# Two alternating groups in the chunk recurrence of a hybrid decoder layer, with copies shared by two engines

## The chip, the cores and the metric

The kernel runs on one core of a Trainium2 chip. The metric is the device time of one execution in microseconds (us). The kernel before was timed in three runs; a fourth execution was profiled.

## The reference, cut to what matters

One decoder layer on a sequence of T = 2048 tokens of width D = 1024, all in float32. Three branches (A, B, C) work on one projection of the normalised input:

```python
h = rms_norm(x, norm_g[l])
p = h @ w_in[l]
y_a = rwkv7_mix(p_r, p_k, p_v, p_w, p_a, ...) * silu(z_a)          # branch A: 8 heads x 64
y_b = sliding_window_sink_attn(p_q, p_sk, p_sv, ...) * silu(z_b)   # branch B: window 128
y_c = memory_cross_attn(p_xq, mem, ...) * silu(z_c)                # branch C: 256 memory tokens
merged = gates[0] * (y_a @ w_proj_a) + gates[1] * (y_b @ w_proj_b) + gates[2] * (y_c @ w_proj_c)
x = x + merged @ w_out
```

Branch A is a recurrence over tokens with a 64x64 state S for each head:

```python
sa = jnp.einsum('bhvk,bhk->bhv', S, a_t)
S = S * w_t[:, :, None, :] + sa[..., None] * b_t[:, :, None, :] + v_t[..., None] * k_t[:, :, None, :]
y = jnp.einsum('bhvk,bhk->bhv', S, r_t)
```

## The kernel before

**Tiling.** The sequence is cut into four blocks of 512 tokens (block 0 to block 3). Most of TensorE's time goes into projections: each 128-row block of weights is split into a high and a low part in a fast format, and three large products of 512 columns (L462 to L464, in `gemm3`) give the projection. Weights come in tiles `whl` of 512 KB, of which a ring holds nine; one tile serves twelve large products. In block 0 the raw weights (256 KB a tile) are loaded, split by ScalarE (L444, a cast) and VectorE (L445), and the split tile is written back to memory (`k`); blocks 1 to 3 load the split tiles.

**The recurrence.** Branch A is computed in chunks of 64 tokens, eight chunks in a block, for eight heads in four pairs. `rwkv_prep` makes four factors for each pair and stores them in memory (`f`); `rwkv_chain` walks through the chunks with all four pairs at once. For each chunk it loads the factors (L852, into `whl` tiles, two chunks' worth being in flight) and runs:

- L866: the W products from the state Z into a PSUM tile `rw` (8 products), L867: the part of the output that depends on Z (8 products, into `yps`);
- L869: VectorE copies W out of PSUM;
- L874: the U products from W (8 products); in odd chunks L845 adds the previous chunk's U part to the output (8 products);
- L877: VectorE copies U into Z in two halves of 64 partitions;
- L879: the S products, the new state (8 products); in odd chunks L845 again, for this chunk;
- L885: VectorE adds the decayed old state SP (made by GpSimd, L872) into a new Z, in two halves; ScalarE copies the output out of PSUM after odd chunks (L889).

Each small float32 product appears in the trace as two records. L866, L867 and L879 use TensorE in the shape 128*64, L874 and L845 in the shape 64*64, and the large products in 128*128. L861 and L862 (GpSimd) fill the halves of Z that come from the values.

**What sets the order.** The program is written as streams (recurrence `r`, attention `a`, merges `b` and `c`, gates `g`), and the letters of `TURNS` say which stream takes the next step, in block 0 and in the blocks after it. Then `order` lays the whole program out again: `lay_out` keeps one clock for each engine and always places the instruction that can start first (on a tie of candidates, the one with the lowest rank, which after the first of `PASSES` = 3 rounds is the latest time at which it is due). Each engine then executes its instructions strictly in the resulting order. `burst` chains the products of a stage behind each other, without a bond to the next stage, so that large products may stand in between. A **visit** below is an unbroken row of the recurrence's products between two other instructions of TensorE.

The order also shows the other small products of TensorE (transposes, attention, the factors' own products): they too make visits, outside the change.

## Time and profile before

| | |
|---|---|
| median of three runs | 2276.46 us (2273.06 to 2279.18) |
| profiled execution, its time | 2280.36 us |
| its span | 2278.6 us |
| recurrence, block 0 | 444 to 510 us |
| recurrence, blocks 1, 2, 3 | 1009 to 1072, 1561 to 1624, 2112 to 2176 us |

The profile has, among others, a list of the engines' busy time, the chain of waits that ended last, groups of instructions by line with their mean length, a table of who waited for whom, a timeline, and windows (stretches of the span with each engine's busy time, the clock granted to TensorE, the share of the DMA engines and what they moved). A record of a matmul is longer than the distance to the next one, since matmuls are pipelined: what a product costs TensorE is read from one start to the next. PEld are TensorE's weight loads.

### The profile page before, as it was taken

What the parts mean: (1) busy time and instruction counts of PE and PEld (TensorE: products, weight loads), DVE (VectorE), ACT (ScalarE), POOL (GpSimd) and SP (SyncE); (2) the same over time, 40 slices, a digit from 0 to 9 for tenths busy, and PEclk for the clock granted to TensorE, in tenths of its full rate; (3) what the DMA queues carried; (4) which work ended last, traced back from release to release, by engine and by line L of the source; (5) the groups of instructions that cost most, each with busy time, mean ns of one, the idle gap of its engine ahead of it and who ended that gap; (6) DMA issues with size and microseconds to landing.
All of it is one profiled execution on the core that took longest, in us unless ns stands there. A gap on an engine that the chain in (4) does not pass through costs nothing.

```text
span 2278.6 us, 38340 instructions
## 1 busy us (share of the span) xinstructions
PE 2236.3 (98%) x14088; PEld 1824.9 (80%) x14088; DVE 1468.4 (64%) x4444; ACT 835.2 (37%) x1803; POOL 212.3 (9%) x297
## 2 busy tenths in 40 slices
PE   7999999999999999999999999999999999999999
PEld 5888888877788888887888788887788878888787
DVE  6789888648468857743627876772454787765252
ACT  5555546326234343311413443421332334251030
POOL 1001000021000100101100000101200000000110
PEclk9999999999999999999999999999999999999999
DMA  7787777877866555567674554556676465546665
GB/s 244 255 273 244 253 248 264 272 249 269 304 237 191 172 171 184 168 202 251 231 245 158 185 188 168 181 170 213 238 241 222 154 193 177 168 154 210 217 216 184
DMA packets 218075, 487.81 MB, mean 214 GB/s; under 512 B 19616, under 2 KB 81440, under 8 KB 217888
## 3 DMA queue, kind: packets, MB, share of 16 engines
q1 hardware_dynamic: 205216, 462.28, 60.3%
q10 hardware_dynamic: 12672, 23.07, 3.0%
q8 instruction: 112, 1.84, 0.3%
q14 instruction: 75, 0.61, 0.1%
HBM read 357.88 MB, written 127.40 MB: 213 GB/s over the span
## 4 chain that ended last, share of the span: by engine, by line
PE 87%; DMA 5%; DVE 5%; ACT 2%; issue 1%; SPq 0%; POOL 0%; ACTq 0%; DVEq 0%
PE mm L462 21%; PE mm L463 21%; PE mm L464 21%; PE rw L758 2%; DMA whl<-in_w_in 2%; PE oo L1085 1%; PE mm L1131 1%; PE mm L1130 1%; PE mm L1132 1%; PE oo L980 1%; DMA whl<-k 1%; DMA rt<-in_x 1%; PE rw L879 1%; PE rw L866 1%; DVE whl L445 1%; PE rw L874 1%
## 5 line engine op out<-in xcount | busy, mean ns | idle before, releaser
L462 PE MATMUL mm<-hH,whl 128*128 128x512 f32 x1888 | 749.1, 397 | 7.5 <-ACT whl L444 5.6
L463 PE MATMUL mm<-hL,whl 128*128 128x512 f32 x1888 | 748.9, 397 | 0.0
L464 PE MATMUL mm<-hH,whl 128*128 128x512 f32 x1888 | 744.8, 395 | 0.0
L462 PEld LDWEIGHTS mm<-hH,whl 128*128 128x128 f32 x1888 | 355.2, 188 | 80.9 <-ACT whl L444 6.3
L463 PEld LDWEIGHTS mm<-hL,whl 128*128 128x128 f32 x1888 | 355.3, 188 | 73.4 <-issue 1.2
L464 PEld LDWEIGHTS mm<-hH,whl 128*128 128x128 f32 x1888 | 355.4, 188 | 71.3 <-DVE whl L445 1.9
L1096 ACT ACTIVATE g<-mm 128x512 f32<-128x512 f32 x96 | 57.4, 598 | 298.3 <-PE mm L464 294.7
L444 ACT ACTIVATE whl<-whl 128x512 fp32r<-128x512 f32 x174 | 109.0, 629 | 149.7 <-DMA whl<-in_w_in 95.0
L445 DVE TENSOR_TENSOR whl<-whl 128x512 fp32r<-128x512 f32 x174 | 119.3, 688 | 68.2 <-ACT whl L444 63.6
L777 DVE TENSOR_TENSOR ibc<-ibc,Yi 128x248 f32<-128x248 f32 (+30 forms) x496 | 143.7, 290 | 11.1
L776 DVE STREAM_SHUFFLE ibc<-Nc 128x248 f32<-128x248 f32 (+30 forms) x496 | 150.8, 312 | 0.1
L462 PE MATMUL mm<-yh,whl 128*128 128x512 f32 x384 | 150.0, 394 | 0.8 <-ACT yh L927 0.5
L464 PE MATMUL mm<-yh,whl 128*128 128x512 f32 x384 | 150.0, 391 | 0.8 <-DVE whl L445 0.8
L463 PE MATMUL mm<-yl,whl 128*128 128x512 f32 x384 | 149.9, 391 | 0.3 <-DVE yl L928 0.2
L778 DVE TENSOR_TENSOR Yi<-Yi,ibc 128x248 f32<-128x248 f32 (+30 forms) x496 | 140.4, 283 | 1.3
L427 POOL TENSOR_SCALAR st<-st 128x4 f32<-128x4 f32 (+1 forms) x32 | 9.7, 303 | 997.1 <-DVE st L513 955.3
L1111 DVE SCALAR_TENSOR_TENSOR g<-g,mm 128x512 f32<-128x512 f32 x64 | 43.7, 685 | 84.2 <-PE mm L464 80.9
L1065 ACT ACTIVATE g<-g,mxs,st 128x256 f32<-128x256 f32 (+1 forms) x128 | 74.4, 583 | 53.3 <-DVE mxs L1058 34.7
L462 PEld LDWEIGHTS mm<-yh,whl 128*128 128x128 f32 x384 | 72.0, 188 | 17.5 <-ACT yh L927 1.3
L463 PEld LDWEIGHTS mm<-yl,whl 128*128 128x128 f32 x384 | 72.1, 188 | 16.0 <-DVE yl L928 1.5
L464 PEld LDWEIGHTS mm<-yh,whl 128*128 128x128 f32 x384 | 72.1, 188 | 15.6 <-DVE whl L445 1.0
L1144 DVE SCALAR_TENSOR_TENSOR g<-mm,g 128x512 f32<-128x512 f32 x16 | 11.0, 690 | 83.4 <-PE mm L1132 78.0
(1734 smaller groups left out, 3492.1 us busy)
## 6 DMA issues: line engine op xcount, KB each, us to landing
whl<-k SPq DMA_DIRECT2D x474, 512.0 KB, 3.4
k<-whl SPq DMA_DIRECT2D x158, 512.0 KB, 3.2
whl<-f SPq DMA_DIRECT2D x128, 256.0 KB, 4.4
whl<-in_w_in SPq DMA_DIRECT2D x118, 256.0 KB, 3.5
f<-FT SPq DMA_DIRECT2D x48, 512.0 KB, 4.8
f<-FT SPq DMA_DIRECT2D x32, 256.0 KB, 4.1
g<-in_x ACTq DMA_DIRECT2D x32, 256.0 KB, 5.5
out<-g ACTq DMA_DIRECT2D x32, 256.0 KB, 4.2
```

The source lines that it names most:

```text
L444: S.activation(w[:, 0], raw, AF.Copy)
L445: V.tensor_tensor(w[:, 1], raw, w[:, 0].bitcast(F32), op=ALU.subtract)
L462: PE.matmul(out, lh, rh, start=i == 0, stop=False)
L463: PE.matmul(out, lh, rl, start=False, stop=False)
L464: PE.matmul(out, ll, rh, start=False, stop=i == n - 1)
L758: PE.matmul(g[:, c], BK[h, c0 + c], Q[h, c0 + c], start=True, stop=True)
L776: V.stream_shuffle(bc[:, :, :n], Nc[:, :, s + 1:], [s] * 32)
L777: V.tensor_tensor(bc[:, :, :n], bc[:, :, :n], Y[:, :, s:s + 1].to_broadcast([128, NC_, n]), op=ALU.mult)
L778: V.tensor_tensor(Y[:, :, s + 1:], Y[:, :, s + 1:], bc[:, :, :n], op=ALU.add)
L1065: S.activation(prs[b][:, i, m0:], prs[b][:, i, m0:], AF.Exp, scale=r2[:, b, i:i + 1], bias=mx[:, b, i:i + 1], accum_out=mx[:, b, 2 + i:3 + i])
L1096: S.activation(t, gp, AF.Tanh, scale=0.5)
L1111: V.scalar_tensor_tensor(g, g, 1.0, pp, op0=ALU.add, op1=ALU.mult)
```

## The change

In `rwkv_chain`, the four pairs are cut into two groups of two (A: pairs 0 and 1, B: pairs 2 and 3). Each stage is written as group A's four products, then group B's, each group with a PSUM half tile of its own and copies of its own. W is copied by ScalarE instead of VectorE (one copy of 128x128 for each group). U is copied by VectorE for the even heads and by ScalarE for the odd heads (64x128 each). The additions of the new state stay on VectorE, now four of 64x128 for each chunk instead of two of 64x256. The next chunk's Z, and GpSimd's copies into it, are made before the S products, and Z has three buffers instead of two. The tile `w4` in `rwkv_prep` has one buffer instead of two.

All of the recurrence's products of a block form one line in a fixed order (`run`, `lines`). In `lay_out`, once a product of the line is placed, its follower (`then`) is preferred: if it can start within `HOLD` = 300 ns of TensorE's clock, it is placed next and TensorE waits for it; if what it depends on isn't placed yet but another engine can place something by then, TensorE places nothing until that is done; otherwise the bond is dropped and large products come in. The planner takes 80 ns instead of 200 as the delay after a product of the line (`late`). The letters of `TURNS` are new.

Line numbers shift: L462 to L464 become L474 to L476, L444 and L445 become L456 and L457, L866 and L867 become L894 and L895, L874 becomes L903, L845 becomes L857, L879 becomes L911, L885 becomes L912, L889 becomes L922, L1096 becomes L1130. The W copy is L896, the U copies are L904 on both engines.

On TensorE, in block 1, an odd chunk of the recurrence before (names: `rw` W, U or S in PSUM, `yps` the output, `mm` a projection):

```order
L866 MATMUL rw<-Z,whl 64x64 x8
L867 MATMUL yps<-Z,whl 64x64 x8
L462 MATMUL mm<-hH,whl 128x512
L874 MATMUL rw<-W,whl 64x64 x8
L845 MATMUL yps<-Z,whl 64x64 x8
L463 MATMUL mm<-hL,whl 128x512
L464 MATMUL mm<-hH,whl 128x512
L462 MATMUL mm<-hH,whl 128x512
L879 MATMUL rw<-Z,whl 64x64 x8
L845 MATMUL yps<-Z,whl 64x64 x8
L463 MATMUL mm<-hL,whl 128x512
```

and an odd chunk of the change, from the first product of the visit:

```order
L894 MATMUL rw<-Z,whl 64x64 x4
L895 MATMUL yps<-Z,whl 64x64 x4
L894 MATMUL rw<-Z,whl 64x64 x4
L895 MATMUL yps<-Z,whl 64x64 x4
L903 MATMUL rw<-W,whl 64x64 x8
L857 MATMUL yps<-Z,whl 64x64 x8
L911 MATMUL rw<-Z,whl 64x64 x8
L857 MATMUL yps<-Z,whl 64x64 x8
L894 MATMUL rw<-Z,whl 64x64 x4
L475 MATMUL mm<-hL,whl 128x512
L476 MATMUL mm<-hH,whl 128x512
```

Before, the chunk is three visits with large products between them; now it is one visit of 52 products that ends with group A's first stage of the next chunk.

On ScalarE, in block 0, a stretch of the recurrence before (casts of weights, gates, output copies):

```order
L444 ACTIVATE whl<-whl 128x512
L889 ACTIVATE rt<-yps 128x128 x4
L444 ACTIVATE whl<-whl 128x512 x2
L1096 ACTIVATE g_5361<-mm 128x512
L444 ACTIVATE whl<-whl 128x512
L889 ACTIVATE rt<-yps 128x128 x4
L1096 ACTIVATE g_5471<-mm 128x512
L444 ACTIVATE whl<-whl 128x512 x2
```

and the beginning of the recurrence in the change:

```order
L896 ACTIVATE W<-rw 128x128
L456 ACTIVATE whl<-whl 128x512
L1130 ACTIVATE g_5140<-mm 128x512
L456 ACTIVATE whl<-whl 128x512
L896 ACTIVATE W<-rw 128x128
L904 ACTIVATE Z<-rw 64x2x64
L456 ACTIVATE whl<-whl 128x512
L904 ACTIVATE Z<-rw 64x2x64
L1130 ACTIVATE g_5188<-mm 128x512
L456 ACTIVATE whl<-whl 128x512
```

The casts of weights (now L456) stand between the new copies of W and U. In the whole recurrence of block 0 there are 16 of them between the first W copy and the last output copies.

The diff, with its two long tables of letters as they are:

```diff
--- before.py
+++ after.py
@@ -20,10 +20,11 @@
 TB = 512
 NG = 12
 NRT = 6
+HOLD = 300
 PASSES = 3
 TURNS = (
-    "rrararaaaraaabaaaaaraaabrrraaaaabacbrbgaaaararrabrbaaabraabgaaararraararcccccccrggrrgrgrrgrrrrgrrc",
-    "aarrbraraaaaraaaaaaaraaaraararbgbaaabracararabaaarrbbabraaaabararaarrgracgcccccrgrgrcrgrrgrrrrrrgc",
+    "rraaaraaaaaaabaraarraaabrarraaaabraabbgaaarcarrbrraaaabbabagaaararaaarccrccrgccrgccrgrrgrgrrgrrrrr",
+    "arraaaaaaaraaarraaaaabbrrggabrbabargaaaaraaararacaarrbbbbaaaraaararaaarcrcccrcggcrrgrrgrgrrrrrrrcc",
 )
 RING = 9
 C = 64
@@ -56,10 +57,11 @@
 
     def __init__(self, ins, masks):
         self.ins, self.eng = ins, NAMES[ins.engine]
+        self.late = LAT[self.eng]
         self.reads, self.writes = ([self.region(a.bass_ap, masks) for a in aps if getattr(a, "bass_ap", None) is not None]
                                    for aps in (ins.ins, ins.outs))
         self.reads, self.writes = ([r for r in l if r] for l in (self.reads, self.writes))
-        self.before, self.after, self.opens, self.end, self.held = set(), [], [], None, set()
+        self.before, self.after, self.opens, self.end, self.held, self.then = set(), [], [], None, set(), None
         self.bytes = 512 * self.n((self.writes + self.reads)[0]) if self.is_dma() else 0
         getattr(self, "cost_" + ("SP" if self.bytes else self.eng))()
 
@@ -194,7 +196,7 @@
 
         if b.eng == s.eng:
             return 0 if s.eng == "PE" else b.end + 30
-        return b.end + LAT[s.eng]
+        return b.end + s.late
 
     def room(s):
 
@@ -222,19 +224,24 @@
     for s in todo:
         if not missing[s]:
             offer(s)
-    tile, fp32, wires = (128, 128), 0, 0
+    tile, fp32, wires, then = (128, 128), 0, 0, None
     for _ in todo:
-        best = None
-        for e, rs in ready.items():
-            if rs:
-                at = max(clock[e], min(rs.values()))
-                if best is None or at < best[0]:
-                    best = at, e
-        at, e = best
+        firsts = {e: max(clock[e], min(rs.values())) for e, rs in ready.items() if rs}
+        if then:
+            hold = clock["PE"] + HOLD
+            if ready["PE"].get(then, hold + 1) <= hold:
+                firsts["PE"] = max(clock["PE"], ready["PE"][then])
+            elif "PE" in firsts and then not in ready["PE"] and any(at <= hold for e, at in firsts.items() if e != "PE"):
+                del firsts["PE"]
+            elif "PE" in firsts:
+                then = None
+        e = min(firsts, key=firsts.get)
+        at = firsts[e]
         can = [s for s, t in ready[e].items() if t <= at]
         s = min(can, key=lambda s: s.rank)
         if e == "PE":
-            s = min(can, key=lambda s: (fp32 and s.tile != tile, s.rank))
+            s = then or min(can, key=lambda s: (fp32 and s.tile != tile, s.rank))
+            then = s.then
             if s.tile != tile:
                 at += 95
             clock[e] = at + s.busy
@@ -293,14 +300,19 @@
         if s in following and s.eng == "PE":
             t = min(t, due[following[s]] - max(s.busy, following[s].end - following[s].dur - (s.end - s.dur) if s.eng == "PE" and False else s.busy))
         for a in back.get(s, ()):
-            t = min(t, due[a] - s.dur - (0 if a.eng == s.eng == "PE" else 30 if a.eng == s.eng else LAT[a.eng]))
+            t = min(t, due[a] - s.dur - (0 if a.eng == s.eng == "PE" else 30 if a.eng == s.eng else a.late))
         due[s] = t
     return due
 
 
-def order(tc, manual):
+def order(tc, manual, lines):
 
     todo = steps(list(tc.nc.cur_bb.bb.instructions), manual)
+    byname = {s.ins.name: s for s in todo}
+    for l in lines:
+        for a, b in zip(l, l[1:]):
+            byname[a].then = byname[b]
+            byname[b].late = 80
     tries = []
     for _ in range(PASSES):
         orders = lay_out(tc, todo)
@@ -352,7 +364,7 @@
     def o_ps():
         return ps.tile([128, 512], F32, name="oo", bufs=1)
 
-    manual = {}
+    manual, lines = {}, []
 
     def behind(later, earlier, done=False):
 
@@ -696,7 +708,7 @@
         bk = BK.rearrange("p c (s t) -> p c s t", t=C)
         kp = proj(B_K + p, hT)
         k = shift(kp, B_K + p, pcol("mu_k", p), dcol("omu_k", p), sb, "rk_")
-        w4 = xp.tile([128, 4, 128], F32R, name="w4", bufs=2)
+        w4 = xp.tile([128, 4, 128], F32R, name="w4", bufs=1)
         nc.sync.dma_start(w4.bitcast(F32), LRd[:, :, p * 128:(p + 1) * 128])
         pw, pa = rw_ps(), rw_ps()
         for d, o in enumerate((pw, pa)):
@@ -835,7 +847,7 @@
         ycs = [tmp() for _ in range(n)]
 
         def states():
-            Z = rp.tile([128, n, 2, C], F32, name="Z", bufs=2)
+            Z = rp.tile([128, n, 2, C], F32, name="Z", bufs=3)
             return Z, ((Z[EV, :, 0], EV), (Z[OD, :, 1], OD))
 
         def yslot(i, c, e):
@@ -852,41 +864,63 @@
                     nc.sync.dma_start(Fs[-1][:, u], group[j + u][1][:, c])
             return lambda i, u: Fs[i // 2][:, i % 2, u]
 
-        Z, halves = states()
+        G2 = [(slice(j, j + 2), [x for x in HH if x[0] in (j, j + 1)]) for j in range(0, n, 2)]
+        line = []
+
+        def run(ms, after=()):
+            burst(ms, line[-1] if line else None, after)
+            line.extend(ms)
+
+        def half():
+            return rw_ps()[:, :2 * C].rearrange("p (i t) -> p i t", i=2)
+
+        def start(c):
+            Z, halves = states()
+            G.tensor_copy(Z[OD, :, 0], Vs[OD, :, c])
+            G.tensor_copy(Z[EV, :, 1], Vs[EV, :, c])
+            return Z, halves
+
+        Z, halves = start(0)
         for z, h in halves:
             S.activation(z, Sst[h], AF.Copy)
-        upds, old, after = [], None, factors(0)
+        upds, old, after = [()] * len(G2), None, factors(0)
         for c in range(NC_):
             g, after = after, factors(c + 1) if c < NC_ - 1 else None
-            G.tensor_copy(Z[OD, :, 0], Vs[OD, :, c])
-            G.tensor_copy(Z[EV, :, 1], Vs[EV, :, c])
             if c % 2 == 0:
                 yps = ps.tile([128, n, 2, C], F32, name="yps", bufs=1)
-            pw = rw_ps()[:, :n * C].rearrange("p (i t) -> p i t", i=n)
-            prev = burst([PE.matmul(pw[h, i], g(i, 1 + 2 * e)[:, :C], Z[:, i, e], start=True, stop=True) for i, e, h in HH], None, upds)
-            burst([PE.matmul(yslot(i, c, e), g(i, 1 + 2 * e)[:, C:], Z[:, i, e], start=i == 0 and c % 2 == 0, stop=False) for i, e, h in HH], prev)
             W = rp.tile([128, n, C], F32, name="W", bufs=1)
-            V.tensor_copy(W, pw)
+            for q, (js, hh) in enumerate(G2):
+                pw = half()
+                run([PE.matmul(pw[h, i % 2], g(i, 1 + 2 * e)[:, :C], Z[:, i, e], start=True, stop=True) for i, e, h in hh], upds[q])
+                run([PE.matmul(yslot(i, c, e), g(i, 1 + 2 * e)[:, C:], Z[:, i, e], start=i == 0 and c % 2 == 0, stop=False) for i, e, h in hh])
+                S.activation(W[:, js], pw, AF.Copy)
             SP = rp.tile([128, n, C], F32, name="SP", bufs=1)
             for z, h in halves:
                 G.tensor_tensor(SP[h], z, Pl[h, sb % 2, :, c:c + 1].to_broadcast([64, n, C]), op=ALU.mult)
-            pu = rw_ps()[:, :n * C].rearrange("p (i t) -> p i t", i=n)
-            prev = burst([PE.matmul(pu[h, i], g(i, 2)[h, :C], W[h, i], start=True, stop=True) for i, e, h in HH])
+            upds = []
+            for js, hh in G2:
+                pu = half()
+                run([PE.matmul(pu[h, i % 2], g(i, 2)[h, :C], W[h, i], start=True, stop=True) for i, e, h in hh])
+                upds.append([V.tensor_copy(halves[0][0][:, js], pu[EV]), S.activation(halves[1][0][:, js], pu[OD], AF.Copy)])
             if c % 2:
-                prev = burst(from_u(c - 1, *old), prev)
-            upds = [V.tensor_copy(z, pu[h]) for z, h in halves]
-            pS = rw_ps()[:, :n * C].rearrange("p (i t) -> p i t", i=n)
-            prev = burst([PE.matmul(pS[h, i], g(i, 0)[:, e * C:(e + 1) * C], Z[:, i, e], start=True, stop=True) for i, e, h in HH], prev, upds[1:])
+                run(from_u(c - 1, *old))
+            new = start(c + 1) if c < NC_ - 1 else None
+            nxt = []
+            for q, (js, hh) in enumerate(G2):
+                pS = half()
+                run([PE.matmul(pS[h, i % 2], g(i, 0)[:, e * C:(e + 1) * C], Z[:, i, e], start=True, stop=True) for i, e, h in hh], upds[q])
+                nxt.append([V.tensor_tensor((new[1][k][0] if new else Sst[h])[:, js], pS[h], SP[h, js], op=ALU.add) for k, h in enumerate((EV, OD))])
+            upds = nxt
             if c % 2:
-                burst(from_u(c, Z, g), prev)
+                run(from_u(c, Z, g))
             old = Z, g
-            if c < NC_ - 1:
-                Z, halves = states()
-            upds = [V.tensor_tensor(z if c < NC_ - 1 else Sst[h], pS[h], SP[h], op=ALU.add) for z, h in halves]
+            if new:
+                Z, halves = new
             yield
             if c % 2:
                 for i in range(n):
                     S.activation(chunks(ycs[i])[:, c - 1:c + 1], yps[:, i], AF.Copy)
+        lines.append([m.ins.name for m in line])
 
         for (p, _, yt), yc in zip(group, ycs):
             mean = xp.tile([128, 8], F32, name="st8", bufs=2)
@@ -1204,7 +1238,7 @@
         if sb + 1 < nsb:
             hT = x_norm(sb + 1)
         output(sb, accs)
-    order(tc, manual)
+    order(tc, manual, lines)
     es.close()
 
 
```

## The prediction

> **What bounds the kernel now.** I read the page's list of engines first, then its chain of waits, then the table of who waited for whom on TensorE.
>
> ```profile
> PE 2236.3 (98%) x14088; PEld 1824.9 (80%) x14088; DVE 1468.4 (64%) x4444; ACT 835.2 (37%) x1803; POOL 212.3 (9%) x297
> PE 87%; DMA 5%; DVE 5%; ACT 2%; issue 1%; SPq 0%; POOL 0%; ACTq 0%; DVEq 0%
> PE mm L462 <- ACT whl L444: 5.9, 4, 2.8
> PE mm L462 <- DMA whl<-k: 0.9, 3, 0.5
> PE as__13354 L525 <- DVE rt L523: 1.4, 1, 1.4
> ```
>
> TensorE is busy for 98% of the span and is 87% of the chain that ends last. Its waits are short and scattered: the second group of rows gives a total, a count and the longest. So time can come only from what TensorE itself does, and the change touches its recurrence products. The groups of instructions by line size them:
>
> ```profile
> L867 PE MATMUL yps<-Z,whl 128*64 128x64 f32 x512 | 21.2, 222 | 0.0
> L874 PE MATMUL rw<-W,whl 64*64 64x64 f32 x512 | 21.8, 224 | 0.1
> L889 ACT ACTIVATE rt<-yps 128x128 f32<-128x128 f32 x64 | 12.8, 280 | 84.4 <-PE yps L845 84.4
> L877 DVE COPY Z<-rw 64x256 f32<-64x256 f32 x64 | 27.0, 422 | 33.1 <-PE rw L874 32.2
> L678 DVE COPY carry<-mm 128x1 f32<-128x1 f32 x52 | 7.8, 149 | 0.0
> ```
>
> Five lines (L866, L867, L874, L879, L845) have 512 records each, two per product. None is removed; what can shrink is the price of interleaving them with the large products of L462 to L464. The timeline of TensorE's matmuls shows that price (start, length, engine and line):
>
> ```profile
> 471.50 0.39 PE L464 MATMUL mm<-hH,whl 128*128 128x512 f32 x1
> 471.82 0.69 PE L866 MATMUL rw<-Z,whl 128*64 128x64 f32 x16
> 472.33 0.64 PE L867 MATMUL yps<-Z,whl 128*64 128x64 f32 x16
> 472.90 0.50 PE L462 MATMUL mm<-hH,whl 128*128 128x512 f32 x1
> 473.33 0.68 PE L874 MATMUL rw<-W,whl 64*64 64x64 f32 x16
> 473.85 0.63 PE L845 MATMUL yps<-Z,whl 64*64 64x64 f32 x16
> 474.41 0.50 PE L463 MATMUL mm<-hL,whl 128*128 128x512 f32 x1
> 474.75 0.39 PE L464 MATMUL mm<-hH,whl 128*128 128x512 f32 x1
> 474.98 0.40 PE L462 MATMUL mm<-hH,whl 128*128 128x512 f32 x1
> 475.31 0.69 PE L879 MATMUL rw<-Z,whl 128*64 128x64 f32 x16
> 475.92 0.68 PE L845 MATMUL yps<-Z,whl 64*64 64x64 f32 x16
> 476.53 0.50 PE L463 MATMUL mm<-hL,whl 128*128 128x512 f32 x1
> 473.33 0.54 PEld L874 LDWEIGHTS rw<-W,whl 64*64 64x64 f32 x16 [0.25 <-issue]
> 473.79 0.55 PEld L845 LDWEIGHTS yps<-Z,whl 64*64 64x64 f32 x16
> ```
>
> Two large products in a row start 0.23 us apart (474.75, 474.98). Sixteen small records take 0.46 us (weight loads of L874 and L845: 473.33 to 473.79). So a visit of TensorE to the recurrence costs, from the large product before it to the next, less one large product and less 0.46 per sixteen records: 472.90 − 471.50 − 0.23 − 0.92 = 0.25 us where it begins with L866; 474.41 − 472.90 − 0.23 − 0.92 = 0.36 where it begins with L874; 476.53 − 474.98 − 0.23 − 0.92 = 0.40 with L879 and then L845.
> ```profile
> 455.37 0.39 PE L462 MATMUL mm<-hH,whl 128*128 128x512 f32 x1
> 455.69 0.69 PE L879 MATMUL rw<-Z,whl 128*64 128x64 f32 x16
> 456.30 0.50 PE L463 MATMUL mm<-hL,whl 128*128 128x512 f32 x1
> ```
>
> With L879 alone it is 456.30 − 455.37 − 0.23 − 0.46 = 0.24, so I put the other 0.15 down to the change of shape inside the visit, from 128*64 to 64*64.
>
> **The change part by part.** *Visits.* The order of TensorE before has 102 visits: 72 begin with L866 or L879, 30 with L874, and 19 shape changes lie inside visits. The new order has 50 visits, one of them beginning with the L874 product, and 74 shape changes inside. Before: 72 × 0.25 + 30 × 0.36 + 19 × 0.15 = 31.7 us. After: 49 × 0.25 + 0.36 + 74 × 0.15 = 23.7 us. The difference is **−8.0 us**. Eight visits of before are split by a single large product; costed as two plain visits, they hide nothing in my favour. Eleven new visits begin with L867's product, which the trace shows nowhere: between 0.25 (taken, its shape is that of L866) and 0.36, 1.2 us more.
>
> The Trainium skill speaks against trading visits for shape changes: in "TensorEngine Tiling (Array Packing)", Tiling Modes, Key Properties, a change of the tiling mode, and not merely of the tile, drains TensorE. If draining meant the whole 222 ns that one small product lasts, 55 more changes would cost 12.2 us instead of 8.3 and the visits would save 4.1. The 0.15 us between the two kinds of visit is a drain only in part, and I keep the row.
>
> *Waits inside a visit.* A longer visit needs its copies in time. One chunk of block 0 before, in which TensorE stayed on the recurrence throughout, shows what they cost (in brackets: idle time before, and what ended it):
>
> ```profile
> 458.34 0.69 PE L866 MATMUL rw<-Z,whl 128*64 128x64 f32 x16
> 459.07 0.42 DVE L869 COPY W<-rw 128x256 f32<-128x256 f32 x1 [1.79 <-PE rw L866]
> 459.55 0.54 PEld L874 LDWEIGHTS rw<-W,whl 64*64 64x64 f32 x16 [0.20 <-DVE W L869]
> 460.35 0.88 DVE L877 COPY Z<-rw 64x256 f32<-64x256 f32 x2 [0.85 <-PE rw L874]
> 461.37 0.69 PE L879 MATMUL rw<-Z,whl 128*64 128x64 f32 x16 [0.67 <-DVE Z L877]
> ```
>
> From the products' end (458.34 + 0.69 = 459.03) to the copy 0.04, from the copy's end (459.49) to TensorE 0.06; after the 64*64 products 0.12 (459.55 + 0.68 = 460.23 to 460.35). TensorE waited 0.20 and 0.67 there, of which 0.15 each is shape change: the change removes these two, **−0.6 us**. All other copies of before are hidden under large products.
>
> Now the new visit. A copy of half width on ScalarE is L889's 0.28 us; on VectorE, 149 ns at one element and 422 at 256 give 0.285 at 128 (estimate from the two rows). Take group A's first product at 0 and 0.23 us for four products. A's W products end at 0.46 (last start 0.23, plus 0.22), ScalarE copies from 0.50 to 0.78, TensorE may go at 0.84. Behind A stand A's output products, B's W products and B's output products until 0.92, and a shape change until 1.07: no wait. B's copy ends at 1.22 and releases at 1.28; A's U products run 1.07 to 1.30: none. A's two half copies, one on each engine, are done at 1.94 (U ends 1.52, + 0.12 + 0.285) and release at 2.00; eight output products and a shape change fill until 2.14. Then A's two additions on VectorE in series: S ends at 2.60, additions until 3.21, release 3.27; B's S products, eight output products and two shape changes fill until 3.36. The cover holds with 0.06 to 0.1 us to spare. That is thin, so I take 0.05 us of wait for each of 16 long visits, **+0.8 us**, with bounds 0 and 0.3 (the planner's HOLD, then 4.8 us). What queues behind a waiting product is the large products behind the visit, and behind those the gates on ScalarE (L1096) and the merges on VectorE. In even chunks three large products stand between U and S, 0.68 us against a copy of 0.46, so nothing waits.
>
> *Engines.* Per chunk VectorE loses W's copy and half of the Z copies, ScalarE gains four copies: 32 × 4 × 0.28 = 36 us on an engine that is busy for 37%. In blocks 1 to 3 the order of ScalarE has only gates and output copies between the new ones, so 0. Halving the instructions does not halve them (0.285 against 0.42), but that time is off TensorE.
>
> *Buffers.* A third Z lets GpSimd fill the next chunk's halves early. One w4 buffer instead of two makes its load wait for the previous pair's L704 products, which lie tens of us earlier in the order; 0, and up to one load's landing if that gap closed.
>
> *Transfers.* Chunks come faster, and each brings its factors. Windows of the trace (length, busy us by engine, then clock, DMA share, GB/s):
>
> ```profile
> 444.00:511.00 67.00, 63.10 (x783) 47.66 (x783) 26.90 (x54) 12.99 (x30) 14.95 (x26) 0.97 0.76 256
> 1008.50:1071.50 63.00, 62.76 (x790) 48.13 (x790) 18.80 (x43) 5.34 (x17) 13.27 (x26) 1.00 0.64 224
> 1024.00:1030.00 6.00, 5.76 (x66) 4.42 (x65) 1.27 (x3) 0.60 (x1) 0.28 (x1) 1.00 0.98 368
> 483.00:486.00 3.00, 0.23 (x8) 0.09 (x4) 0.00 (x0) 0.61 (x1) 0.00 (x0) 1.00 0.98 324
> 486.00:490.00 4.00, 3.93 (x24) 2.69 (x25) 2.19 (x5) 0.64 (x2) 0.00 (x0) 0.71 0.63 252
> 490.00:493.00 3.00, 3.00 (x32) 2.04 (x33) 0.79 (x2) 0.00 (x0) 1.67 (x2) 0.82 0.44 172
> 486.07 0.50 PE L462 MATMUL mm<-hH,whl 128*128 128x512 f32 x1 [2.84 <-ACT whl L444]
> ```
>
> In block 1 the recurrence spans 150 large products before and 83 after: 63 us shrink to about 18.4 (640 records) + 6 (visits) + 83 × 0.23 = 43 us. It moves 63 × 224 = 14.1 MB now; 67 fewer large products are 5.6 weight tiles of 0.52 MB less, so 11.2 MB in 43 us, 260 GB/s, where 368 were reached. That holds: 0, bounds 0 and +3 us (a half us in each pair of chunks in which a tile is late, as L462 waited for whl<-k thrice). In block 0 the span goes from 140 to 192 large products: 67 × 256 = 17.2 MB plus 52 / 12 × 0.79 MB gives 20.6 MB in 18.4 + 6 + 44 = 68 us, 303 GB/s, near the 324 at which TensorE stood still for 2.84 us with the DMA engines 98% busy. The half clock that followed cost 4 × 0.29 + 3 × 0.18 = 1.7 us more. I leave this stall of 4.5 us as it is, with bounds of −4.5 and +4.5.
>
> *The rest of the order.* The numbers that set the turns are new, so everything moves a little. Visits to other small products number 256 before and 253 after: 0, with 4 us either way (L525's wait of 1.4 us stands in three blocks and may go or come).
>
> The sum: −8.0 − 0.6 + 0.8 = **−7.8 us** on the profiled execution's 2280.36, which is 3.9 above the median of the runs; the same on the median 2276.46 is **2268.7 us**.
>
> **The rivals.** *The cover fails by the allowed wait.* Each long visit waits 0.3: −8.0 − 0.6 + 4.8 = −3.8, 2272.7 us. For it: the cover's margin of under 0.1 us. Against: in blocks 1 to 3 no other work of VectorE stands between the recurrence's own instructions. The page's drain, at its dearest, would give the same time (−4.1 − 0.6 + 0.8 = −3.9).
>
> *More is gained than the visits.* The stall at 483 and L525's three waits vanish: −7.8 − 4.5 − 4.2 = −16.5, 2260.0 us. For it: both are accidents of one order. Against: block 0 asks for more bytes per us than before.
>
> *Slower: ScalarE's casts hold the recurrence in block 0.* ScalarE works in order, and there 16 weight casts stand between the new copies.
>
> ```profile
> ACT whl L444 <- DMA whl<-in_w_in: 95.0, 54, 6.1
> ```
>
> A cast that waits for its tile waits 95.0 / 54 = 1.76 us, and now W's copy stands behind it and TensorE behind W. Eight late casts cost 14.1 us and turn −7.8 into +6.3; that is the point from which it decides. With ten: +17.6 − 7.8 = +9.8, 2286.3 us. For it: 303 GB/s. Against: before, only one such wait reached TensorE inside the recurrence, since the order places casts whose tiles are expected.
>
> *The change does not do what it says* is answered by the order: the visits are merged in every block, though in block 0 the first chunk is still broken up by 54 large products.
>
> **How the numbers follow.** About 0.3% (6.8 us) is what a measurement of this kernel can tell from no change; faster means below 2269.6. Forecast 0.48, own range 2263 to 2274, a little over half of it below that line (0.29 faster, 0.18 same, 0.01 slower). Cover fails 0.25 (0.04, 0.20, 0.01). More gained 0.15, all faster. Casts 0.12 (0.01 same, 0.11 slower). Sum: faster 0.48, same 0.39, slower 0.13. The range reaches to the second and third case and part of the way to the fourth: 2257 to 2280.
>
> **What would show it.** Right: visits of 52 products of the recurrence in the timeline of TensorE with no idle time over 0.15 us inside; windows over the recurrence of blocks 1 to 3 shrunk from 63 to about 43 us; the five lines' idle column still near 0. Wrong: waits of these lines for ScalarE's W or VectorE's Z in the table of waits; whl<-f among TensorE's waits; in block 0, L874's successor waiting for W behind a cast; or a shape change from L867 to L874's product dearer than 0.15.

## The result, and the profile after

The change runs in 2261.86 us (2261.22 to 2262.54, four runs) against 2276.66 for the kernel before (four runs, three of them those timed before the change): a ratio of 0.9936, 95% interval 0.9919 to 0.9953. Six more runs on another occasion gave 2261.79 us and 0.992 (0.9904 to 0.9936). So the change is faster by 15 to 19 us, where 8 were forecast. The profiled execution took 2261.22 us with a span of 2259.2, 19.4 us less than the span of before; that execution of before was itself 3.7 us above its median.

The page of the change, list of engines and chain of waits, and its table of who waited for whom on TensorE (total, times, longest):

```profile
PE 2219.8 (98%) x14088; PEld 1824.3 (81%) x14088; DVE 1445.3 (64%) x4476; ACT 873.3 (39%) x1937; POOL 212.7 (9%) x297
...
PE 89%; DMA 4%; DVE 3%; ACT 3%; issue 1%; SPq 0%; ACTq 0%; POOL 0%; DVEq 0%
```
```profile
...
PE mm L474 <- ACT yh L961: 5.1, 3, 3.7
PE mm L474 <- ACT whl L456: 3.1, 4, 1.3
...
PE mm L474 <- DMA whl<-k: 1.3, 2, 0.7
PE rw L911 <- ACT Z L904: 1.0, 4, 0.4
PE rw L894 <- PE yps L857: 0.9, 5, 0.2
...
PE rw L903 <- ACT W L896: 0.8, 1, 0.8
...
PE as__1157 L1010 <- DVE g L1008: 0.7, 1, 0.7
...
PE as__495 L537 <- DVE rt L535: 0.4, 1, 0.4
```

TensorE is still what bounds the kernel. Its waits have changed places. In the same table of before stood these rows beside the one that the prediction shows:

```profile
PE as__18720 L525 <- DVE rt L523: 1.4, 1, 1.4
PE as__7988 L525 <- DVE rt L523: 1.4, 1, 1.4
PE as__7360 L976 <- DVE g L974: 1.3, 1, 1.3
PE as__12726 L976 <- DVE g L974: 1.3, 1, 1.3
PE as__18092 L976 <- DVE g L974: 1.3, 1, 1.3
```

L525 and L976 (now L537 and L1010) are small products of other streams, which waited for VectorE once in each block after block 0. After the change 0.4 and 0.7 us are left of them, in block 0.

To see where the time went, I cut TensorE's time by starts: each matmul record costs the distance to the start of the next. "Recurrence" below is what the five lines' records cost, with what the last record ahead of a visit costs beyond the 0.227 us of a large product. "Rest" is the cost of all other records beyond 0.227 us for each large product (0.12 for each product of 128 rows and 256 columns), so it holds the other small products and every other wait. "Half clock" is the time inside the span in which TensorE was granted half its clock; it costs at most half its length. Recurrence, rest and half clock are of one profiled execution each; medians and ratios are of all runs, each beside runs of the kernel before.

| profiled execution | recurrence, us | rest, us | half clock, us | median, us | ratio (interval) |
|---|---|---|---|---|---|
| before | 113.1 | 319.1 | 6.8 | 2276.66 | 1 |
| the change | 107.6 | 305.6 | 3.4 | 2261.86 | 0.9936 (0.9919 to 0.9953) |
| the change, again | 107.3 | 304.9 | 13.9 | 2261.79 | 0.9920 (0.9904 to 0.9936) |
| change, letters of before | 113.1 | 325.9 | 22.1 | 2285.91 | 1.0035 (1.0022 to 1.0047) |
| before, new letters | 118.7 | 320.6 | 28.3 | 2291.08 | 1.0054 (1.0040 to 1.0068) |
| change without the line | 132.8 | 305.1 | 23.9 | 2288.92 | 1.0044 (1.0031 to 1.0056) |
| one group | 110.3 | 308.7 | 6.8 | 2268.85 | 0.9964 (0.9951 to 0.9976) |
| copies on VectorE | 114.9 | 307.6 | 17.1 | 2269.95 | 0.9965 (0.9954 to 0.9977) |
| HOLD = 0 | 111.1 | 307.9 | 14.1 | 2265.89 | 0.9936 (0.9920 to 0.9952) |
| HOLD = 600 | 110.0 | 307.7 | 6.8 | 2267.37 | 0.9946 (0.9931 to 0.9961) |
| one pair of letters exchanged | 107.9 | 305.1 | 10.2 | 2264.76 | 0.9946 (0.9933 to 0.9959) |
| additions by group | 108.0 | 305.1 | 10.4 | 2260.50 | 0.9921 (0.9907 to 0.9935) |
| additions by group, again | 107.4 | 305.5 | 7.9 | 2262.70 | 0.9923 (0.9907 to 0.9938) |
| and U in two tiles | 107.3 | 308.2 | 17.1 | 2261.19 | 0.9933 (0.9921 to 0.9945) |

So between these two executions 5.5 us came from the recurrence and 13.5 from the rest; 10.9 of these 13.5 lie in the steps from a large product to another stream's small product (27.4 us before, 16.5 after), where the six waits were.

One long visit of the change in block 1 (start, length, engine and line; in brackets idle time and what ended it):

```profile
1029.51 0.40 PE L474 MATMUL mm<-hH,whl 128*128 128x512 f32 x1
...
1029.84 0.45 PE L894 MATMUL rw<-Z,whl 128*64 128x64 f32 x8
...
1030.58 0.40 PE L895 MATMUL yps<-Z,whl 128*64 128x64 f32 x8
...
1030.92 0.68 PE L903 MATMUL rw<-W,whl 64*64 64x64 f32 x16
...
1031.43 0.63 PE L857 MATMUL yps<-Z,whl 64*64 64x64 f32 x16
1031.48 0.48 DVE L904 COPY Z<-rw 64x128 f32<-64x128 f32 x2 [1.80 <-PE rw L903]
1031.86 0.44 ACT L904 ACTIVATE Z<-rw 64x128 f32<-64x128 f32 x2 [0.78 <-DVE Z L904]
...
1032.18 0.69 PE L911 MATMUL rw<-Z,whl 128*64 128x64 f32 x16
...
1032.80 0.68 PE L857 MATMUL yps<-Z,whl 64*64 64x64 f32 x16
...
1033.66 0.45 PE L894 MATMUL rw<-Z,whl 128*64 128x64 f32 x8 [0.18 <-PE yps L857]
...
1034.04 0.50 PE L475 MATMUL mm<-hL,whl 128*128 128x512 f32 x1
1032.75 1.02 DVE L912 TENSOR_TENSOR Z<-rw,SP 64x128 f32<-64x128 f32 x4 [0.79 <-PE rw L911]
```

From 1029.51 to 1034.04 are 4.53 us; less one large product (0.23) and 13 times 0.23 for 52 products, 1.31 are left, where the prediction's prices give 0.25 + 4 × 0.15 = 0.85 and 0.05 of wait. Two places hold the difference. The S products (L911) wait for ScalarE's half copies of U, which start only when VectorE's copy from the same PSUM tile is done: its 0.78 us of idle time end with "DVE Z L904". And group A's next W products (L894) come 0.86 us after the 16 records ahead of them, because VectorE's four additions (L912) run in the order A even, B even, A odd, B odd, so that A's product waits for the third. A change of shape without a wait costs what was forecast: 1030.58 to 1030.92 is 0.11 more than eight records, and the next 16 take 0.05 more, 0.16 in all.

Block 0 has a new stall, 30 us behind the recurrence. TensorE's timeline and a window of the change, and a window of before (length, busy us by engine, clock, DMA share, GB/s):

```profile
548.10 0.39 PE L476 MATMUL mm<-yh,whl 128*128 128x512 f32 x1
552.23 0.73 PE L474 MATMUL mm<-yh,whl 128*128 128x512 f32 x2 [3.74 <-ACT yh L961]
```
```profile
541.00:557.00 16.00, 9.83 (x32) 5.84 (x31) 9.42 (x16) 9.02 (x18) 1.84 (x2) 0.89 0.88 302
```
```profile
545.00:557.00 12.00, 11.38 (x48) 8.12 (x46) 9.81 (x20) 6.99 (x18) 1.59 (x2) 1.00 0.84 300
```

TensorE works 9.83 of 16 us there, where before lost 0.62 of 12. The recurrence of block 0 now ends at 516.7 us (510.7 before), and the merge products need its output through a chain on ScalarE and VectorE (the stall ends with `yh`); no other product stands ahead of them in TensorE's order. The profile's own chain of waits also passes here through a transfer of raw weights (`whl<-in_w_proj`, 3.14 us, landed at 547.65) and their cast and split, so that transfers may have a part in it; no run separates the two. The stall is like the one at 483 us of before, with one stretch of half clock each.

### The profile page after: what moved, and what is told of

Same layout as the page of the kernel before. It is cut to its first block, busy times and chain, and to the rows that moved or that the text cites. A ratio compares the mean times of both kernels' runs of the same rounds, so it can differ in the third digit from the quotient of the medians.

```text
span 2259.2 us, 38547 instructions
## 1 busy us (share of the span) xinstructions
PE 2219.8 (98%) x14088; PEld 1824.3 (81%) x14088; DVE 1445.3 (64%) x4476; ACT 873.3 (39%) x1937; POOL 212.7 (9%) x297
## 4 chain that ended last, share of the span: by engine, by line
PE 89%; DMA 4%; DVE 3%; ACT 3%; issue 1%; SPq 0%; ACTq 0%; POOL 0%; DVEq 0%
PE mm L474 22%; PE mm L475 21%; PE mm L476 21%; PE rw L770 2%; PE oo L1119 1%; DMA whl<-in_w_in 1%; PE mm L1165 1%; PE mm L1166 1%; PE mm L1164 1%; PE oo L1014 1%; PE rw L911 1%; DMA rt<-in_x 1%; PE rw L894 1%; PE rw L716 1%; PE rw L903 1%
## 5 line engine op out<-in xcount | busy, mean ns | idle before, releaser
L474 PE MATMUL mm<-hH,whl 128*128 128x512 f32 x1888 | 747.8, 396 | 3.5 <-ACT whl L456 1.8
L476 PE MATMUL mm<-hH,whl 128*128 128x512 f32 x1888 | 742.1, 393 | 0.4 <-DVE whl L457 0.2
L474 PEld LDWEIGHTS mm<-hH,whl 128*128 128x128 f32 x1888 | 354.7, 188 | 77.4 <-ACT whl L456 4.5
L476 PEld LDWEIGHTS mm<-hH,whl 128*128 128x128 f32 x1888 | 354.8, 188 | 72.5 <-DVE whl L457 2.7
L1130 ACT ACTIVATE g<-mm 128x512 f32<-128x512 f32 x96 | 57.4, 598 | 296.1 <-PE mm L476 295.7
L457 DVE TENSOR_TENSOR whl<-whl 128x512 fp32r<-128x512 f32 x174 | 120.4, 696 | 80.2 <-ACT whl L456 74.6
L456 ACT ACTIVATE whl<-whl 128x512 fp32r<-128x512 f32 x174 | 108.9, 630 | 147.7 <-DMA whl<-in_w_in 88.2
L474 PE MATMUL mm<-yh,whl 128*128 128x512 f32 x384 | 150.4, 394 | 5.6 <-ACT yh L961 5.1
L789 DVE TENSOR_TENSOR ibc<-ibc,Yi 128x248 f32<-128x248 f32 (+30 forms) x496 | 143.6, 289 | 10.9
L476 PE MATMUL mm<-yh,whl 128*128 128x512 f32 x384 | 150.1, 392 | 0.0
L439 POOL TENSOR_SCALAR st<-st 128x4 f32<-128x4 f32 (+1 forms) x32 | 10.2, 320 | 887.1 <-DVE st L525 887.1
L474 PEld LDWEIGHTS mm<-yh,whl 128*128 128x128 f32 x384 | 72.2, 188 | 22.6 <-ACT yh L961 6.1
L476 PEld LDWEIGHTS mm<-yh,whl 128*128 128x128 f32 x384 | 72.4, 189 | 14.8
L904 DVE COPY Z<-rw 64x128 f32<-64x128 f32 x64 | 15.4, 277 | 90.4 <-PE rw L903 90.3
```

Of the source, the lines that this page charges most:

```text
L456: S.activation(w[:, 0], raw, AF.Copy)
L457: V.tensor_tensor(w[:, 1], raw, w[:, 0].bitcast(F32), op=ALU.subtract)
L474: PE.matmul(out, lh, rh, start=i == 0, stop=False)
L476: PE.matmul(out, ll, rh, start=False, stop=i == n - 1)
L789: V.tensor_tensor(bc[:, :, :n], bc[:, :, :n], Y[:, :, s:s + 1].to_broadcast([128, NC_, n]), op=ALU.mult)
L1130: S.activation(t, gp, AF.Tanh, scale=0.5)
```

## The experiments

**Are the letters or the structure the gain?** First the change with the letters of before, then before with the new letters. The diff is the table `TURNS` alone:

```diff
 TURNS = (
-    "rraaaraaaaaaabaraarraaabrarraaaabraabbgaaarcarrb..."   # change
+    "rrararaaaraaabaaaaaraaabrrraaaaabacbrbgaaaararra..."   # before
```

> The change with the letters of TURNS of before; all else as changed. Its order has 51 visits of the recurrence (102 before, 50 in the change) and 267 other visits (256 and 253). Theory A (most of the gain is in the rest of the order, which the letters set): the visits' gain stays and the rest goes back, so 5 to 8 us under before: 2268 to 2272 us. Rival B (the shorter recurrence itself gives the whole gain by freeing engines and buffers): the time of the change, 2260 to 2265 us.

> The kernel before with the letters of TURNS of the change, nothing else. Its order has 95 visits of the recurrence and 246 other visits. Theory A (letters set the rest of the order): 8 to 13 us under before, 2263 to 2269 us. Rival B (letters are worth nothing without the shorter recurrence): 2274 to 2280 us, as before.

Measured: 2285.91 and 2291.08 us, both slower than before and all theories missed. Their rows in the tables of waits, the change with old letters first:

```profile
PE as__13482 L537 <- DVE rt L535: 1.4, 1, 1.4
PE as__18912 L537 <- DVE rt L535: 1.4, 1, 1.4
PE as__8052 L537 <- DVE rt L535: 1.4, 1, 1.4
PE as__12854 L1010 <- DVE g L1008: 1.3, 1, 1.3
PE as__7424 L1010 <- DVE g L1008: 1.3, 1, 1.3
PE as__18284 L1010 <- DVE g L1008: 1.3, 1, 1.3
```
```profile
PE as__1157 L976 <- DVE g L974: 0.7, 1, 0.7
```

With the old letters the six waits are there, with the new ones they are gone, whatever the recurrence is. So they belong to the letters. But neither half is worth anything alone. On the program that the letters were not made for, TensorE was at half clock for 22 to 28 us, up to 11 to 14 us of cost. And with the new letters on the kernel before, its rest is 320.6 us, not less than the 319.1 of before: other waits (3.3 us for `yh` is the longest) and the half clock take the place of the six.

**What is the line worth?** Groups, shared copies and letters are kept; no product of the recurrence is bound to its follower.

```diff
-    order(tc, manual, lines)
+    order(tc, manual, [])
```

> The change without the line that TensorE holds to (no follower, no waiting up to HOLD, 200 ns assumed after a product again); two groups, ScalarE's copies and the new letters stay. Its order has 103 visits of the recurrence and 47 shape changes inside them: 103 x 0.25 + 26 x 0.11 + 47 x 0.15 = 35.7 us against the 33.7 us that the 50 visits of the change cost with their waits. Theory A (the line is what saves visits, but waits inside eat most of it): 1 to 5 us over the change, 2263 to 2267 us. Rival (two groups and ScalarE's copies give the gain, the line nothing): equal to the change within 1 us, or faster.

Measured: 2288.92 us. The direction is the theory's, the size is not: 27 us against 1 to 5. The rest is the same to half a us (305.1 and 305.6), so nearly all of it is the recurrence: 132.8 instead of 107.6 in 103 visits instead of 50. Part of that can be the clock. Windows of this kernel (columns as above) and a row of its timeline:

```profile
1604.00:1608.60 4.60, 3.14 (x55) 2.26 (x57) 0.98 (x4) 1.19 (x6) 2.02 (x4) 1.00 0.99 362
1608.60:1622.30 13.70, 13.70 (x139) 9.46 (x133) 2.86 (x10) 1.92 (x7) 1.24 (x2) 0.50 0.25 89
```
```profile
1606.75 0.50 PE L474 MATMUL mm<-hH,whl 128*128 128x512 f32 x1 [1.44 <-DMA whl<-k]
```

A wait of 1.44 us for a tile, in a stretch of small products, is followed by 13.7 us at half clock in which TensorE is never idle. At most (23.9 − 3.4) / 2 = 10 us of the 25 are clock; the other 15 are visits and their waits.

**How much HOLD?** The line stays, and only how long TensorE may wait for it changes.

```diff
-HOLD = 300
+HOLD = 0        # other run: 600
```

> The change with HOLD = 0 instead of 300: TensorE follows the line only where the next product can start at once by the planner's clock. The order has 67 visits with 54 shape changes instead of 50 with 74 (most long visits break into one up to the U products and one that begins with S); visits to other small products 253, as in the change. Theory (a visit costs 0.25 us, a shape change 0.15, and a long visit of the change holds 0.4 us of waits that large products would cover here): 17 more visits are +4.3, 20 fewer changes -3.0, and about 12 fewer waits of 0.19 and of 0.22 us are -4.9, so -3.6: about 2258, 2256 to 2262, no slower than the change. Rival (the allowed wait is worth its price, since what it saves is more than visits, by way of the order around it): slower than the change by over 5 us, 2267 or more.

> The change with HOLD = 600 instead of 300: 51 visits with 73 shape changes, 252 visits to other small products, nearly the order of the change; one long visit more ends before group A's first stage of the next chunk. Theory: by visits and waits no difference, 2260 to 2264. Rival (any relaying of the order loses several us, since the letters were fitted to one order): 2265 or more.

Measured: 2265.89 and 2267.37 us. For HOLD = 0 both expectations are missed: steps inside the recurrence got cheaper (93.5 to 87.0 us), as the theory says, but what it saves there is paid at entries (+3.6) and at exits (+6.5), where there are 17 visits more and the large product behind a visit waits more often for its tile:

```profile
PE mm L474 <- DMA whl<-k: 4.1, 5, 1.4
```

(1.3 in 2 in the change; four of these five waits stand behind a visit.) For HOLD = 600 the time agrees with the rival, that a relaid order costs some us by itself. By the intervals neither is told apart from the first measurement of the change. So it is not the wait of up to 300 ns that does the work of the line. What is left is the preference for the follower and the planner's 80 ns instead of 200 after a product, which the run without the line gave up together; no run tells these two apart.

**How much do two groups and ScalarE's copies give?** In the first run all four pairs are one group (line, ScalarE and letters kept), in the second W and the odd U halves are copied by VectorE.

```diff
-        G2 = [(slice(j, j + 2), [x for x in HH if x[0] in (j, j + 1)]) for j in range(0, n, 2)]
+        G2 = [(slice(0, n), HH)]
```
```diff
-                S.activation(W[:, js], pw, AF.Copy)
+                V.tensor_copy(W[:, js], pw)
...
-                upds.append([..., S.activation(halves[1][0][:, js], pu[OD], AF.Copy)])
+                upds.append([..., V.tensor_copy(halves[1][0][:, js], pu[OD])])
```

> The change with all four pairs in one group again (stages of eight products, W's copy 128x256 on ScalarE, U's halves 64x256 on VectorE and ScalarE, two additions of 64x256); the line that TensorE holds to and the new letters stay. Its order has 61 visits of the recurrence and 52 shape changes (50 and 74 in the change), other visits 253 as there. What the visits cost beyond 0.0288 us a record was 39.3 us before, 33.7 in the change and 58.9 without the line. Theory (the line does most of it; the groups only cover the copies): 61 x 0.25 + 52 x 0.15 = 23 us and waits of 0.15 to 0.3 at each of 31 W copies and 0.6 at four U copies, 31 to 36 us; total within 5 us of the change, 2260 to 2267. Rival (without the second group the copies lie open and TensorE is starved as without the line): over 45 us, total 2275 or more.

> The change with W's copies and U's odd halves on VectorE again; groups, line and letters stay. Its order has 64 visits and 69 shape changes. Theory (ScalarE's share is needed for the cover; VectorE in order delays the copies): 64 x 0.25 + 69 x 0.15 = 26 us and waits, 36 to 45 us for the visits, total 2264 to 2272. Rival (VectorE is free enough in the recurrence, so that ScalarE's share is worth nothing): 31 to 35 us, total 2260 to 2264.

Measured: 2268.85 and 2269.95 us, 7 and 8 us slower than the change. For the copies that is inside the theory's range and above the rival's; for the groups it lies just above the theory's and well below the rival's. But every such edit lays the whole order out anew, and in the recurrence itself the groups are worth 2.7 us (110.3 against 107.6) and ScalarE's copies 7.3 (114.9 against 107.6); the rest of the two differences lies in the order around it and, with the copies on VectorE, in 17.1 us of half clock. In one group, the timeline shows a whole copy on each engine, one behind the other (in the same PSUM tile):

```profile
1033.50 0.42 DVE L904 COPY Z<-rw 64x256 f32<-64x256 f32 x1 [4.41 <-PE rw L903]
...
1034.01 0.38 ACT L904 ACTIVATE Z<-rw 64x256 f32<-64x256 f32 x1 [1.36 <-DVE Z L904]
```

With the copies on VectorE, the table of waits shows what is late instead:

```profile
PE rw L894 <- DVE Z L912: 4.1, 14, 0.3
...
PE rw L911 <- DVE Z L904: 2.3, 5, 0.8
```

**The two waits inside a long visit.** First VectorE's finished order is changed only in that the four additions of a chunk, where they stand side by side, come as A even, A odd, B even, B odd. Then, in addition, the odd heads' U products get a PSUM tile of their own, so that the two engines read different tiles.

```diff
+    place = {s: k for k, s in enumerate(orders["DVE"])}
+    for quad in quads:
+        q = [byname[x] for x in quad]
+        ks = sorted(place[s] for s in q)
+        if ks[3] - ks[0] == 3:
+            orders["DVE"][ks[0]:ks[0] + 4] = q
```
```diff
-                pu = half()
+                pu, pv = half(), s_ps()[:, :2 * C].rearrange("p (i t) -> p i t", i=2)
...
-                upds.append([..., S.activation(halves[1][0][:, js], pu[OD], AF.Copy)])
+                upds.append([..., S.activation(halves[1][0][:, js], pv[OD], AF.Copy)])
```

> The change with its final order kept on every engine but for VectorE's four additions of a chunk, which now stand A-even, A-odd, B-even, B-odd instead of A-even, B-even, A-odd, B-odd. Theory (in the 11 long visits group A's next product waits for its second addition, which stands third): the step from L857's last product to the next L894 product falls from 0.36 to 0.40 us to about 0.15, 11 x 0.22 = 2.4 us less: 2259.5 us. Rival (the 0.36 us is TensorE's own price for going from the shape 64*64 back to 128*64): no change, 2261.9 us.

> The change with VectorE's additions by group (as in the run before this one) and with U's products of odd heads written to a PSUM tile of their own (the pool as_), so that ScalarE's copy of the odd half no longer waits for VectorE's copy of the even half. Theory (the step of 0.34 us from L857 to the S products in odd chunks is the two half copies one behind the other): the step falls to 0.15, about 15 x 0.19 = 2.8 us less than with additions by group: 2257.7 us. Rival (the step is a price of the shape): unchanged, 2260.5.

The timelines of both show each wait removed, additions by group first, then with two tiles:

```profile
1033.93 0.68 PE L863 MATMUL yps<-Z,whl 64*64 64x64 f32 x16
...
1034.60 0.45 PE L900 MATMUL rw<-Z,whl 128*64 128x64 f32 x8
```
```profile
1036.87 0.27 PE L909 MATMUL rw<-W,whl 64*64 64x64 f32 x1
...
1037.42 0.48 DVE L910 COPY Z<-rw 64x128 f32<-64x128 f32 x2 [1.55 <-PE as__11060 L909]
1037.44 0.27 ACT L910 ACTIVATE Z<-as__11060 64x128 f32<-64x128 f32 x1 [0.41 <-PE as__11060 L909]
...
1037.95 0.69 PE L917 MATMUL rw<-Z,whl 128*64 128x64 f32 x16
```

(L863, L900, L909, L910, L917 are L857, L894, L903, L904, L911 of the change.) From the output's U part to group A's next products 0.67 us instead of 0.86; from the U products to S 1.08 instead of 1.26, with both engines' copies starting 0.02 us apart. With 11 and 16 such places that is 2.1 and 2.9 us, and over the whole profiles the 11 steps fell from 4.2 to 1.9 us and the 16 from 5.8 to 2.5. The time doesn't show it: 2260.5 and 2261.19 us. With the additions by group the steps inside the recurrence fell from 93.5 to 91.0 us, but the exits rose from 9.3 to 12.0. In the second run the recurrence's 107.3 us hold 1.2 us of waiting for nothing that the profile shows, at 1064, and the rest is 2.6 us longer. So the waits are what I say they are, and taking them away isn't worth their sum: for the additions, what is saved inside is waited for at the exits; for the two tiles this is likely, but the other changes of that order hide it.

**How much does any new order cost or bring?** Two letters (61 and 62 of the second table) are exchanged:

```diff
-    "...aarrbbbbaaaraaararaaarcrcccr..."
+    "...aarrbbbbaaaaraararaaarcrcccr..."
```

> The change with two neighbouring letters of the second table exchanged (an r and an a, the 61st and 62nd); nothing else. The recurrence keeps its 50 visits and 74 shape changes; other visits become 259 from 253. Theory (the letters are fitted to just this program, and what the rest of the order costs moves by several us with any edit): 3 to 15 us over the change, 2265 to 2277. Rival (neighbouring tables are as good, and the slow mixes of the last runs were slow because whole tables were foreign): within 2 us, 2260 to 2264.

Measured: 2264.76 us, between the two. Then the change and the additions by group once more, side by side:

> The change once more, beside the variant with the additions by group, so that small differences between the variants are read against runs of one chip and one hour. Theory (the variants with HOLD = 0, HOLD = 600 and one pair of letters exchanged really are 3 to 5 us slower than the change): ratio to before 0.991 to 0.9935, some 2258 to 2263 where before is near 2278. Rival (the change is no faster than they are, and its first median was a little low): ratio 0.994 or more, 2264 or more.

> The additions of the new state put by group (A even, A odd, B even, B odd) in VectorE's order, nothing else. Theory (the wait of group A's product for the third addition costs 0.2 us in each of 11 long visits): 1.5 to 3 us faster than the change on the same chip. Rival (what is saved is waited for elsewhere): within 1 us of it.

Measured: 2261.79 us (0.992) and 2262.70 us (0.9923). The theory's number for the change holds; that HOLD = 0, HOLD = 600 and the exchanged letters are really slower is not shown by it, since their intervals reach into that of the change. For the additions the rival does: their first 2260.5 was no gain that repeats, and the same trade shows again (steps inside 94.1 to 91.1, exits 8.4 to 11.5 us). No variant beats the change.

## Why the prediction was right, and where not

**The forecast** was 2268.7 us with 2257 to 2280: right in sign and inside the range, below the likeliest case's own 2263 to 2274. The total of −7.8 us was about half of what came, and two of its terms were wrong in opposite directions. That the time still lies inside the range is partly luck: the visits, from which the whole forecast came, brought some 2.5 us net of their waits, and most of the gain came from a term that the forecast put at 0 ± 4.

**Visits, −8.0.** The count of visits and the price of a shape change hold (0.16 us against 0.15). By the row, the rule cited from the Trainium skill ("TensorEngine Tiling (Array Packing)", Tiling Modes) holds as a partial drain, not as a whole small product.

**New waits inside visits, +0.8.** This is a step that failed. The prediction let group A's two half copies of U run at once on two engines, and put A's two additions first and second on VectorE. Neither is so: 16 × 0.18 + 11 × 0.19 = 5.0 us, just over the upper bound of 4.8, but for other reasons than HOLD. With it and the one wait for W (0.8 us) the steps give −7.8 − 0.8 + 5.0 + 0.8 = −2.8. Measured are −5.5, of which 3.0 is the wait at 483 us that vanished; 2.5 is left for the visits. The named sign for this was idle time over 0.15 us inside a long visit, and it is there.

**The wait at 483 us, left as it was.** It is gone from the recurrence, and its like stands at 548 us. The runs don't show that one caused the other.

**The rest of the order, 0 ± 4.** The largest miss: −13.5. The prediction had L525's three waits as what "may go"; the three of L976, as regular, it did not count. Together they are 8.1 us in the table of waits, and the two runs with exchanged letters show them to come and go with the letters. But on the kernel before, the new letters removed them without any gain in the rest, so the six waits alone don't explain the 13.5. Why less came in their place in the change stays open, and so does the remaining 5 us, which is spread over small places.

**Transfers, 0.** Right inside the recurrence; for the stall at 548 us it is open. Windows of the change, the first over the stretch of block 0 that the prediction shows of before, the second over the recurrence of block 1:

```profile
444.00:511.00 67.00, 64.59 (x708) 50.60 (x707) 22.60 (x60) 20.78 (x59) 14.29 (x26) 1.00 0.85 286
1012.40:1059.00 46.60, 44.93 (x724) 35.88 (x723) 12.79 (x49) 11.97 (x47) 12.59 (x24) 1.00 0.65 222
```

Block 1 takes 46.6 us instead of the forecast 43, at 222 GB/s instead of 260. Block 0 takes 74.4 us (442.3 to 516.7) instead of the forecast 68, 286 GB/s in the window instead of 303. Waits for `whl<-k` are 1.3 us in all, for `whl<-f` none.

**The rivals.** "More is gained than the visits", 2260.0 us with a chance of 0.15, came nearest, and by two of its own pieces: the stall at 483 and L525's waits went. It should have had more than 0.15, and L976. "The cover fails" was right about the place and nearly about the sum, but the other gain hid it. ScalarE's casts held the recurrence once, 0.84 us before L903, not eight times.

**The buffers** of w4 and the third Z were not tried apart: what each gives or costs is not shown.

## What to carry to other kernels

Merging visits of small products pays by the visit, but the sum must follow every copy to the tile that it reads and every addition to its real place in its engine's order, or the waits inside the new visit eat more than half of it (5.0 of 8.0 us here). Where a planner lays out a whole program from a table, the table and the program are one change: each half alone was slower than before here. Regular waits, here of 1.3 and 1.4 us, that return once in each block are the first place to look for what a new order may bring.

## What the runs showed of the hardware

**The half clock can last longer than what starts it.** Stretches at half clock were 3.4, 6.8, 10.2 or 13.7 us long in all kernels (the last one aside, where the program ends). The Trainium skill ("TensorE: Matmul & The Clock Gate", Part 1) has the clock judged in free-running windows of 3.4 us, and the lengths agree. The Trainium skill there lets an idle window bring the half clock and a busy one end it. The run without the line agrees with neither: in the 3.4 us ahead of the half clock (1605.20 to 1608.61) TensorE was busy for 1.97, with one wait of 1.44 us, and 13.7 us without an idle moment in the profile passed before the full clock came back. The length of the wait alone doesn't decide: in the kernel before, six waits of 1.3 to 1.4 us and one of 2.15 us at 602, in stretches of large products, brought no half clock. That the small products around the wait make the difference is likely, but no run shows it. Nor does the time at half clock tell the loss: the change's second profile has 13.9 us of it and a span of 2258.6, since much of it falls into the stall at 548 us:

```profile
548.30:552.00 3.70, 1.34 (x4) 0.53 (x2) 2.54 (x4) 2.98 (x6) 0.00 (x0) 0.50 0.73 204
552.00:558.50 6.50, 5.70 (x13) 4.04 (x14) 4.11 (x8) 3.30 (x8) 0.00 (x0) 0.50 1.02 394
```

**Two engines don't copy out of one PSUM tile at once in this program.** In the change none of ScalarE's 64 half copies began before VectorE's of the same group had ended. In 31 cases ScalarE sat idle until then, 25.5 us in all, most of it from before the products of U were done:

```profile
its engine sat idle before it (us, times) until:
  PE rw L903: 90.3, 26
  DVE Z L904: 25.5, 31
```

With a tile for each engine 62 of the 64 overlapped. All 64 copies of the change wait for a semaphore that VectorE's copies raise and start 62 ns or more after it, so the order probably comes from the program and not from the chip; that the chip would copy both halves of one tile at once, no run shows.
